# A SwiGLU encoder block on one core: the first gate/up pair with its loads by halves and an order of its own

## The chip, the cores and the metric

The kernel runs on one core of a Trainium2 chip. A core has a matrix engine (PE, TensorE), a vector engine (DVE, VectorE), a scalar engine (ACT, ScalarE), GpSimd (POOL), and SyncE (SP), which here only issues transfers (DMA). Each engine works through its own list of instructions in order; semaphores make one engine wait for another. Matrix products accumulate in PSUM banks and are read from there by VectorE or ScalarE. The metric is the device time of one execution, in microseconds, and the runs of the kernel before scatter between 2363.36 and 2370.91.

## The reference

One block of a streaming encoder, in float32: a SwiGLU feed-forward of half weight, a token mixer and a second SwiGLU feed-forward, each with a residual and a layer norm. `D_MODEL` and the sequence are 1024, the feed-forward width is 4096.

```python
def swiglu(x, w_gate, w_up, w_down):
    return (jax.nn.silu(x @ w_gate) * (x @ w_up)) @ w_down

    x = layer_norm(DN_ALPHA * x + 0.5 * swiglu(x, ffn1_w_gate, ffn1_w_up, ffn1_w_down), ln1_g, ln1_b)
    z = x @ w_in
    # fox: 8 heads of forgetting attention on z;  lru: causal convolution and a gated linear recurrence on z
    x = layer_norm(DN_ALPHA * x + concatenate([fox, lru]) @ w_out, ln2_g, ln2_b)
    x = layer_norm(DN_ALPHA * x + 0.5 * swiglu(x, ffn2_w_gate, ffn2_w_up, ffn2_w_down), ln3_g, ln3_b)
```

The part that matters here is `x @ w_gate` and `x @ w_up` at the start of both feed-forwards, FFN1 and FFN2.

## The kernel before

**Precision.** Each float32 operand is held in two parts. [...] One step of a product is three matmuls into one bank, high by high (L155), high by low (L156) and low by high (L157), in `mm3`. A low part needs its high part, so every operand passes VectorE (or a transpose on TensorE), ScalarE and VectorE again: L242/L243 for blocks of x, L293/L294 for blocks of weights.

**Products.** The feed-forwards' gate and up matrices are taken in 16 pairs of 256 columns each. For a pair, `x` (1024 x 1024) and the weights (1024 x 256) are cut into 2 x 2 blocks, and seven products of Strassen's kind (Winograd's form) replace eight: one (w11 by x11), two (w21 by x12), six (t2 by s2), five (t1 by s1), seven (t3 by s3), three (w22 by s4) and four (t4 by x22). s1 to s4 are sums and differences of blocks of x and stay for all 16 pairs; t1 to t4 are differences of weight blocks, made anew for each pair. Each product is 4 steps of 3 matmuls on 512 columns. So a pair is 14 products, seven for gate and seven for up.

**Pair 0 of FFN1.** x comes in by rows of 128 tokens, rows 0 to 3 on SP's queue, rows 4 to 7 on POOL's, each a whole row of 512 KB; then the gate and the up weights, 1 MB each, on SP. A row must be transposed on TensorE (4 transposes for half a row) before it can be a block. `blocks_1` makes the blocks "11" and "12" from rows 0 to 3. `blocks_2` makes, for each of the four groups j of tokens, s1 and "22" from row 4+j, and in a later pass s2, s3 and s4 together, each by an operation of VectorE (L260, L266, L268, L270) on what the step ahead left. It is a generator: `gate_up` advances it, and the generators of both matrices' weights, between the products, in the order one, two, five, four, six, seven, three. This order is not binding: a scheduler orders the instructions of every engine by their expected readiness.

**Buffers.** Raw weights go into two tiles (pool `rawp`), one for gate and one for up, so the load of pair 1's gate weights can be issued only when pair 0's last reader of its gate tile is through. Parts of weights take 16 tiles of pool `gu_ws`, differences 4 tiles of `gu_t`; products and transposes take turns in six PSUM banks, and two more hold running sums. Results and x's rows live in eight row tiles.

**After the pairs.** `finish` (L399 and the lines around it) multiplies gate and up of a pair, forms the seven operands of the down projection and stores them over POOL's queue; `down_ffn` then runs the down projection. FFN2 follows the mixer, its rows are the results of the second layer norm, and the transposes of "11" and "12" are spread among the mixer's last output tiles.

## Time and profile before

| what | value |
| --- | --- |
| median of 3 runs | 2370.35 us |
| the runs | 2363.36 to 2370.91 us |
| the profiled execution | 2369.74 us |
| its span | 2368.0 us |
| granted TensorE clock, mean | 0.993 |
| TensorE, busy | 2311.0 us |
| VectorE, busy | 1630.8 us |
| ScalarE, busy | 1010.8 us |
| GpSimd, busy | 224.0 us |

The profiled execution is one run of its own, 1.74 us longer than its span of instructions. A row of a view by time reads: start in us, busy us, engine, line, operation, output<-input, shapes, count, and in brackets the idle time of that engine just before it, with what ended it. Names are shortened there to their letters: `b` is a PSUM bank, `x` one of the two sum banks, `raw` a raw weight tile, `ws` a tile of `gu_ws`, `t` a difference of weights, `A` a block "11", "12" or "22", `As` a block s1 to s4, `row` one of the row tiles. A matmul's 0.39 us reaches from its start to its end in the pipeline; the next one starts 0.23 us after it.

### The profile page before, as it was taken

How to read it: one execution, taken by the hardware profiler on the slowest of the kernel's cores; microseconds unless marked ns; L12 is line 12 of the kernel's file. 1: busy time of each engine (PE TensorE's matmuls, PEld its weight loads, DVE VectorE, ACT ScalarE, POOL GpSimd, SP SyncE). 2: the span in 40 equal slices, each digit the busy share in tenths (PEclk: the TensorE clock that was granted, in tenths of full speed). 3: DMA queues.
4: the chain of work that ended last, by engine and by line, in shares of the span. 5: the costliest groups of instructions: out<-in, count | busy, mean ns of one | idle time of the engine just before them, and what ended most of it. 6: DMA issues, size and time to landing. Idle time of an engine off the chain costs nothing.

```text
span 2368.0 us, 28300 instructions
## 1 busy us (share of the span) xinstructions
PE 2311.0 (98%) x10709; PEld 1920.8 (81%) x10709; DVE 1630.8 (69%) x2512; ACT 1010.8 (43%) x1587; POOL 224.0 (9%) x368
## 2 busy tenths in 40 slices
PE   7999999999999999899999899999999999999997
PEld 6888888888788888788888787888888888788886
DVE  7766565666567786866657899766656565577787
ACT  5443433434344344454446745434333433344341
POOL 0020000000000000111133510000000000000000
PEclk9999999999999999999999999999999999999999
DMA  3433232323365432233365911423323232564532
GB/s 111 137 97 116 91 127 85 116 85 116 139 244 207 166 109 93 73 106 101 110 181 134 250 58 57 134 85 116 105 96 116 90 128 86 183 246 167 196 107 89
DMA packets 175768, 298.93 MB, mean 126 GB/s; under 512 B 8128, under 2 KB 100608, under 8 KB 175632
## 3 DMA queue, kind: packets, MB, share of 16 engines
q1 hardware_dynamic: 151984, 216.06, 28.8%
q0 software_dynamic: 23648, 81.07, 9.3%
q8 instruction: 84, 1.38, 0.2%
q14 instruction: 52, 0.43, 0.1%
HBM read 214.22 MB, written 82.87 MB: 125 GB/s over the span
## 4 chain that ended last, share of the span: by engine, by line
PE 87%; DVE 7%; issue 3%; ACT 1%; DMA 1%; POOL 1%; SPq 0%; POOLq 0%; ACTq 0%; DVEq 0%
PE x L156 9%; PE x L157 9%; PE x L155 9%; PE b L156 7%; PE b L157 7%; PE b L155 7%; PE s L157 6%; PE s L155 6%; PE s L156 6%; PE a L156 6%; PE a L157 6%; PE a L155 6%; PE a L880 1%; DMA raw<-in_ffn_w_gate_dram 1%; PE a L864 1%
## 5 line engine op out<-in xcount | busy, mean ns | idle before, releaser
L293 ACT CAST ws<-t 128x512 fp32r<-128x512 f32 x256 | 159.0, 623 | 397.8 <-PE b L156 268.7
L294 DVE TENSOR_TENSOR ws<-raw,ws 128x512 fp32r<-128x512 f32 x192 | 132.1, 688 | 145.2 <-ACT ws L293 141.8
L293 ACT CAST ws<-raw 128x512 fp32r<-128x512 f32 x192 | 118.8, 622 | 264.2 <-PE x L156 256.9
L294 DVE TENSOR_TENSOR ws<-t,ws 128x512 fp32r<-128x512 f32 x256 | 175.7, 687 | 70.4 <-ACT ws L293 68.4
L155 PE MATMUL x<-As,ws 128*128 128x512 f32 x512 | 200.0, 391 | 4.4 <-ACT As L242 4.4
L155 PE MATMUL a<-ws,ws 128*128 128x512 f32 x512 | 199.3, 391 | 3.2 <-ACT ws L487 3.2
L156 PE MATMUL a<-ws,ws 128*128 128x512 f32 x512 | 200.6, 392 | 0.6 <-DVE ws L488 0.5
L156 PE MATMUL x<-As,ws 128*128 128x512 f32 x512 | 200.2, 391 | 0.5 <-DVE As L243 0.4
L157 PE MATMUL a<-ws,ws 128*128 128x512 f32 x512 | 200.6, 392 | 0.0
L155 PE MATMUL b<-As,ws 128*128 128x512 f32 x512 | 199.7, 390 | 0.2 <-ACT row L354 0.2
L157 PE MATMUL x<-As,ws 128*128 128x512 f32 x512 | 199.9, 390 | 0.0
L157 PE MATMUL b<-As,ws 128*128 128x512 f32 x512 | 199.5, 390 | 0.0
L156 PE MATMUL b<-As,ws 128*128 128x512 f32 x512 | 199.5, 390 | 0.0
L155 PE MATMUL x<-A,ws 128*128 128x512 f32 x496 | 193.9, 391 | 4.2 <-ACT ws L293 3.9
L157 PE MATMUL x<-A,ws 128*128 128x512 f32 x496 | 193.9, 391 | 1.3 <-DVE ws L294 1.3
L156 PE MATMUL x<-A,ws 128*128 128x512 f32 x496 | 193.6, 390 | 0.0
L487 ACT CAST ws<-raw 128x1024 fp32r<-128x1024 f32 x112 | 117.3, 1049 | 174.1 <-PE a L156 90.6
L488 DVE TENSOR_TENSOR ws<-raw,ws 128x1024 fp32r<-128x1024 f32 x112 | 136.6, 1221 | 63.3 <-ACT ws L487 62.6
L409 POOL DMA_DIRECT2D h_d<-row x96 | 68.2, 713 | 1159.5 <-DVE row L403 1119.9
L155 PE MATMUL s<-ws,ws 128*128 128x512 f32 x384 | 149.6, 390 | 0.0
L157 PE MATMUL s<-ws,ws 128*128 128x512 f32 x384 | 149.6, 389 | 0.0
L156 PE MATMUL s<-ws,ws 128*128 128x512 f32 x384 | 149.5, 389 | 0.0
(232 smaller groups left out, 5206.7 us busy)
## 6 DMA issues: line engine op xcount, KB each, us to landing
raw<-h_d SPq DMA_DIRECT2D x56, 1024.0 KB, 5.5
h_d<-row POOLq DMA_DIRECT2D x96, 512.0 KB, 3.7
raw<-in_ffn_w_gate_dram SPq DMA_DIRECT2D x32, 1024.0 KB, 5.5
raw<-in_ffn_w_up_dram SPq DMA_DIRECT2D x32, 1024.0 KB, 5.5
wd<-in_ffn_w_down_dram SPq DMA_DIRECT2D x32, 1024.0 KB, 7.8
h_d<-row POOLq DMA_DIRECT2D x32, 256.0 KB, 2.6
raw<-in_w_in_dram SPq DMA_DIRECT2D x16, 512.0 KB, 5.1
row<-in_x_dram SPq DMA_DIRECT2D x12, 512.0 KB, 9.4
```

Of the source, the lines that this page charges most:

```text
L155: mm(out, ah, bh, start=first, stop=False, skip_group_check=goes_on)
L156: mm(out, ah, bl, start=False, stop=False, skip_group_check=goes_on)
L157: mm(out, al, bh, start=False, stop=last, skip_group_check=goes_on)
L293: nc.scalar.copy(hi, src)
L294: v.tensor_tensor(lo, src, f32(hi), ALU.subtract)
L409: nc.gpsimd.dma_start(d[:, 2 * n:2 * n + 2], t.rearrange("p (r t) -> p r t", r=2))
L487: nc.scalar.copy(hi, src)
L488: self.mark = v.tensor_tensor(lo, src, f32(hi), ALU.subtract)
L864: nc.tensor.transpose(pa[:, (j % 4) * P:(j % 4 + 1) * P], p[:, j * P:(j + 1) * P], self.ident)
L880: mm(pv[:, ps], vt[:, j, :], pts[h, qt][j // 4][l][:, j % 4, ps], start=j == 0 and l == 0, stop=j == last and l == 1)
```

## The change

**Loads.** For FFN1 everything now goes over SP's queue: the first halves (columns 0 to 511) of rows 0 to 3, the first halves (input rows 0 to 511) of the gate and up weights of pair 0, then the second halves of both, then rows 4 to 7 whole. Twelve transposes of the identity matrix into a bank that nobody reads stand at TensorE's start. In FFN2 the weights of pair 0 are loaded by the same two halves.

**Order.** `gate_up` has a function `first_pair` that writes pair 0 out step by step. In FFN1 it runs under `manual_schedule` for TensorE, VectorE and ScalarE: within it these three engines take their instructions in the order in which the program writes them. In FFN2 the same function runs without that and the scheduler orders it. `blocks_2` now makes s1, then s2, s3 and s4 each for all four j, one j at a time, and keeps the four transposed banks of x11 from s2 to s3. In `first_pair` w22 is made last, and t2 and t4 later than t1. In FFN1 x22's parts for j = 0, 1, 2, 3 are made after s1 of j = 0, 1, 3, 3.

**Buffers.** Rows 4 to 7 of FFN1 are in a pool of their own (`x2`), which is closed after s1; s4's block is opened in that place. The parts of w11, w21 and w22 have fixed tiles, the t21 and s tiles of `blocks_2` are eight tiles of `gu_ws`. The sum of products six and five is formed in `m.u` instead of a result row, so pair 0 takes seven row tiles where it took eight. The accumulator's rows are taken in plain order.

The diff, cut to its core:

```diff
-    def blocks_2(self, rows, bank, tmp):
+    def block_1(self, j, half, rows, bank):
+
+        self.block_parts(("11", "12")[half], j, self.transposed(rows, half, bank))
+
+    def blocks_2(self, rows, bank, t21, s):
 
         nc, v = self.nc, self.nc.vector
         r1, r2 = rows[0:4], rows[4:NT]
-        t21, s = [], []
+        a22 = []
         for j in range(4):
-            t21.append(tmp())
-            s.append(tmp())
             nc.scalar.copy(t21[j], self.transposed(r2[j], 0, bank))
-            a22 = self.transposed(r2[j], 1, bank)
-            v.tensor_tensor(s[j], a22, t21[j], ALU.add)
+            a22.append(self.transposed(r2[j], 1, bank))
+            v.tensor_tensor(s[j], a22[j], t21[j], ALU.add)
             self.block_parts("s1", j, s[j])
-            self.block_parts("22", j, a22)
-        yield
+            for k in ((0,), (1,), (), (2, 3))[j]:
+                self.block_parts("22", k, a22[k])
+            yield
+        a11 = []
         for j in range(4):
-            a11, a12 = (self.transposed(r1[j], half, bank) for half in range(2))
-            v.tensor_tensor(s[j], s[j], a11, ALU.subtract)
+            a11.append(self.transposed(r1[j], 0, bank))
+            v.tensor_tensor(s[j], s[j], a11[j], ALU.subtract)
             self.block_parts("s2", j, s[j])
-            v.tensor_tensor(t21[j], a11, t21[j], ALU.subtract)
+            yield
+        for j in range(4):
+            v.tensor_tensor(t21[j], a11[j], t21[j], ALU.subtract)
             self.block_parts("s3", j, t21[j])
+            yield
+        for j in range(4):
+            a12 = self.transposed(r1[j], 1, bank)
             v.tensor_tensor(s[j], a12, s[j], ALU.subtract)
             self.block_parts("s4", j, s[j])
             yield
 
...
+    def first_raws(self, *ws):
+
+        raws = [self.raw([P, KT, 2 * P]) for _ in ws]
+
+        def load(half):
+            ks = slice(4 * half, 4 * half + 4)
+            for r, w in zip(raws, self.gu_views(*ws)):
+                self.nc.sync.dma_start(r[:, ks, :], w[:, ks, 0:2 * P])
+
+        return raws, load
+
...
+        def first_pair(gate, up):
+
+            both = gate, up
+            b = [quarters(r) for r in raws]
+            homes = {n: [two_blocks() for _ in both] for n in ("11", "21")}
+            t21, s = ([block() for _ in range(4)] for _ in range(2))
+            blocks = self.blocks_2(rows, bank, t21, s)
+            t = {}
+
+            def fill(m, n, src):
+                k = both.index(m)
+                m.w[n] = parts(src, homes[n][k] if n in homes else None)
+
+            def steps(n):
+                for _ in range(n):
+                    next(blocks)
+
+            if later:
+                later[0](0)
+            for m, q in zip(both, b):
+                fill(m, "11", q[0])
+            gate.one()
+            for m, q in zip(both, b):
+                t["1", m] = less(q[1], q[0])
+            if later:
+                later[0](1)
+            up.one()
+            for m, q in zip(both, b):
+                fill(m, "t1", t["1", m])
+                fill(m, "21", q[2])
+            for m, q in zip(both, b):
+                t["2", m] = less(q[3], t["1", m])
+            if later:
+                gate.two()
+                steps(1)
+                up.two()
+                steps(3)
+                later[1]()
             else:
-                t2 = less(b22, t1)
-                w["t2"] = parts(t2)
-                w["t1"] = parts(t1)
-                w["t3"] = parts(less(b22, b12))
-                w["22"] = parts(b22)
-                w["t4"] = parts(less(b21, t2))
+                steps(4)
+                gate.two()
+                up.two()
+            x = bank()
+            steps(2)
+            gate.five(x)
+            fill(gate, "t4", less(b[0][2], t["2", gate]))
+            x = bank()
+            steps(2)
+            up.five(x)
+            fill(up, "t4", less(b[1][2], t["2", up]))
+            gate.four_alone()
+            steps(2)
+            fill(gate, "t2", t["2", gate])
+            up.four_alone()
+            steps(2)
+            gate.six_five()
+            fill(up, "t2", t["2", up])
+            homes["22"] = [two_blocks() for _ in both]
+            fill(gate, "t3", less(b[0][3], b[0][1]))
+            up.six_five()
+            steps(2)
+            fill(up, "t3", less(b[1][3], b[1][1]))
+            gate.seven_four()
+            steps(2)
+            up.seven_four()
+            for m, q in zip(both, b):
+                fill(m, "22", q[3])
+            for m in both:
+                m.three_alone()
 
...
                 m.six()
-                v.tensor_tensor(m.c[1], m.u, m.s5, ALU.add)
+                v.tensor_tensor(m.u, m.u, m.s5, ALU.add)
...
             def three_alone(m):
-                v.tensor_tensor(m.c[1], m.product("22", "s4"), m.c[1], ALU.add)
+                v.tensor_tensor(m.c[1], m.product("22", "s4"), m.u, ALU.add)
...
             if pair == 0:
-                blocks = self.blocks_2(rows, bank, block)
-                for x in w:
-                    next(x)
-                gate.one()
-                next(blocks)
-                gate.two()
-                up.one()
-                for x in w:
-                    next(x)
-                up.two()
-                for step in ("five", "four_alone", "six_five", "seven_four", "three_alone"):
-                    for m in (gate, up):
-                        getattr(m, step)()
-                        next(blocks, None)
-                    for x in w:
-                        next(x, None)
+                with self.tc.manual_schedule(engines=ENGINES) if later else nullcontext():
+                    first_pair(gate, up)
...
-        blk.open_blocks(xl, ("s3", "s4", "s1", "s2"))
-        rows = blk.rows()
-        for i in range(NT):
-            if i < 4:
-                nc.sync.dma_start(rows[i], xf[i * P:(i + 1) * P, :])
-            else:
-                nc.gpsimd.dma_start(rows[i], xf[i * P:(i + 1) * P, :])
-        for j in range(4):
-            blk.blocks_1(j, rows[j], bank)
-        finish = blk.gate_up(ffn1_w_gate[0], ffn1_w_up[0], h_d[0], rows, bank, tp, wsp, lambda: blk.mixer_consts(
+        blk.open_blocks(xl, ("s3", "s1", "s2"))
+        rows = [blk.row() for _ in range(4)]
+        x2 = inner.enter_context(ExitStack())
+        xp = x2.enter_context(blk.pool("x2", 4, side="right"))
+        rows += [xp.tile([P, D], F32, tag="x2", name=blk.nm("x2")) for _ in range(4)]
+
+        def open_s4():
+            x2.close()
+            blk.open_blocks(inner.enter_context(blk.pool("s4", side="right")), ("s4",))
+
+        raws, load = blk.first_raws(ffn1_w_gate[0], ffn1_w_up[0])
+        warm = bank()
+        for _ in range(12):
+            nc.tensor.transpose(warm[:, 0:P], blk.ident, blk.ident)
+        for half in range(2):
+            for i in range(4):
+                nc.sync.dma_start(rows[i][:, half * H:(half + 1) * H], xf[i * P:(i + 1) * P, half * H:(half + 1) * H])
+            load(half)
+        for i in range(4, NT):
+            nc.sync.dma_start(rows[i], xf[i * P:(i + 1) * P, :])
+
+        def block_1(half):
+            for j in range(4):
+                blk.block_1(j, half, rows[j], bank)
+
...
-        finish = blk.gate_up(ffn2_w_gate[0], ffn2_w_up[0], h_d[1], rows, bank, tp, wsp)
+        raws, load = blk.first_raws(ffn2_w_gate[0], ffn2_w_up[0])
+        load(0)
+        load(1)
```

Two places of VectorE's list in FFN1's pair 0, before and in the change. The rows of the change have the changed kernel's own line numbers: L239 and L303 are its low parts (L243 and L294 before), L253, L261, L265 and L270 the operations of s1, s2, s3 and s4 (L260, L266, L268 and L270 before), L308 a difference of weights (L299 before).

The first place is the forming of s2 and s3. VectorE before (`ws_237` and `ws_255` are the running s tiles of j = 0 and 1, `ws_236` and `ws_254` the t21 tiles, `As_18` and `As_19` are s2's high and low block, `As_12` and `As_13` s3's, `As_14` and `As_15` s4's; `b` are banks with transposed x):

```order
L266 TENSOR_TENSOR ws_237<-ws_237,b_392 128x512
L268 TENSOR_TENSOR ws_236<-b_392,ws_236 128x512
L294 TENSOR_TENSOR ws_361<-t_358,ws_360 128x512
L243 TENSOR_TENSOR As_19_121<-ws_237,As_18_120 128x4x128
L243 TENSOR_TENSOR As_13_115<-ws_236,As_12_114 128x4x128
L270 TENSOR_TENSOR ws_237<-b_397,ws_237 128x512
L266 TENSOR_TENSOR ws_255<-ws_255,b_425 128x512
L268 TENSOR_TENSOR ws_254<-b_425,ws_254 128x512
L243 TENSOR_TENSOR As_15_117<-ws_237,As_14_116 128x4x128
L243 TENSOR_TENSOR As_19_121<-ws_255,As_18_120 128x4x128
L243 TENSOR_TENSOR As_13_115<-ws_254,As_12_114 128x4x128
L270 TENSOR_TENSOR ws_255<-b_430,ws_255 128x512
```

VectorE at the same place in the change (`ws_183` to `ws_186` are the running s tiles of j = 0 to 3, `As_16` and `As_17` are s2's block, `t_423` and `t_459` are t4 of gate and up):

```order
L261 TENSOR_TENSOR ws_183<-ws_183,b_394 128x512
L239 TENSOR_TENSOR As_17_119<-ws_183,As_16_118 128x4x128
L261 TENSOR_TENSOR ws_184<-ws_184,b_402 128x512
L239 TENSOR_TENSOR As_17_119<-ws_184,As_16_118 128x4x128
L308 TENSOR_TENSOR t_423<-raw_131,t_291 128x512
L303 TENSOR_TENSOR ws_426<-t_423,ws_425 128x512
L261 TENSOR_TENSOR ws_185<-ws_185,b_430 128x512
L239 TENSOR_TENSOR As_17_119<-ws_185,As_16_118 128x4x128
L261 TENSOR_TENSOR ws_186<-ws_186,b_438 128x512
L239 TENSOR_TENSOR As_17_119<-ws_186,As_16_118 128x4x128
L308 TENSOR_TENSOR t_459<-raw_132,t_293 128x512
L303 TENSOR_TENSOR ws_462<-t_459,ws_461 128x512
```

Before, two other instructions stand between an operation and its low part; now each low part stands right behind its operation, and s2 comes as a run of four with t4 between.

The second place is the end of pair 0. VectorE before (`raw_202` and `raw_212` are pair 0's raw tiles of gate and up, `raw_641` is pair 1's of gate, `t_518` and `t_524` are t3, `x` are sums of products):

```order
L294 TENSOR_TENSOR ws_521<-t_518,ws_520 128x512
L299 TENSOR_TENSOR t_524<-raw_212 128x512
L370 TENSOR_TENSOR row_199<-row_198,row_197 128x512
L294 TENSOR_TENSOR ws_527<-t_524,ws_526 128x512
L294 TENSOR_TENSOR ws_559<-raw_202,ws_558 128x512
L370 TENSOR_TENSOR row_200<-row_198,row_197 128x512
L294 TENSOR_TENSOR ws_563<-raw_212,ws_562 128x512
L357 TENSOR_TENSOR row_199<-x_222,row_197 128x512
L374 TENSOR_TENSOR row_194<-row_194,x_222 128x512
L357 TENSOR_TENSOR row_200<-x_322,row_197 128x512
L374 TENSOR_TENSOR row_195<-row_195,x_322 128x512
L294 TENSOR_TENSOR ws_644<-raw_641,ws_643 128x512
```

VectorE there in the change (`raw_131` and `raw_132` are pair 0's raw tiles, `As_82` and `As_83` s4's block, `ws_528` and `ws_530` the low parts of gate's and up's w22):

```order
L308 TENSOR_TENSOR t_567<-raw_132 128x512
L303 TENSOR_TENSOR ws_570<-t_567,ws_569 128x512
L431 TENSOR_TENSOR row_166<-x_219,row_165 128x512
L448 TENSOR_TENSOR row_162<-row_162,x_219 128x512
L270 TENSOR_TENSOR ws_185<-b_587,ws_185 128x512
L239 TENSOR_TENSOR As_83_392<-ws_185,As_82_391 128x4x128
L270 TENSOR_TENSOR ws_186<-b_595,ws_186 128x512
L239 TENSOR_TENSOR As_83_392<-ws_186,As_82_391 128x4x128
L431 TENSOR_TENSOR row_167<-x_265,row_165 128x512
L448 TENSOR_TENSOR row_163<-row_163,x_265 128x512
L303 TENSOR_TENSOR ws_528<-raw_131,ws_527 128x512
L471 TENSOR_TENSOR row_163<-row_163,row_162 128x1024
```

Before, the last readers of the two raw tiles stand right behind t3; now they stand behind the last two operations of s4, their low parts and the additions of product seven.

The third place is SP's queue ahead of FFN2, in the change (`q`, `kh`, `kl`, `v` and `cum` are the last head's tiles of the attention, `mix` the mixer's tiles for its output projection, `raw_12055` the raw tile of FFN2's first up weights):

```order
L885 DMA q_11093<-q_d 64x1024
L886 DMA kh_11094<-k_d 64x1024
L887 DMA kl_11095<-k_d 64x1024
L888 DMA v_11096<-v_d 128x8x128
L890 DMA cum_11092<-cum_d 128x1024
L284 DMA raw_12055<-in_ffn_w_up_dram 128x4x256
L996 DMA mix_11239<-mix_d 128x1024
L996 DMA mix_11240<-mix_d 128x1024
L90 DMA gb_11243<-in_ln_g_dram 128x1024
```

Before, the two weight loads are whole and stand next to each other in front of the last head's loads (`raw_12033` and `raw_12043`, rows 166 and 167 of SP's list); now the up weights' second half stands behind the last head's loads and in front of the mix tiles.

94 lines of the change are left out of this document (45 added, 49 removed).

## The prediction

> **What bounds the kernel now.** I read the page first (busy shares, the chain of waits), then the first 110 us by windows and by time on each engine, because nearly all of the change lies in the first gate/up pair of either FFN.
>
> ```profile
> PE 2311.0 (98%) x10709; PEld 1920.8 (81%) x10709; DVE 1630.8 (69%) x2512; ACT 1010.8 (43%) x1587; POOL 224.0 (9%) x368
> PE 87%; DVE 7%; issue 3%; ACT 1%; DMA 1%; POOL 1%; SPq 0%; POOLq 0%; ACTq 0%; DVEq 0%
> core 0: us, PE busy (x) PEld busy (x) DVE busy (x) ACT busy (x) POOL busy (x), PEclk, DMA share, GB/s
> 10.00:20.00 10.00, 5.15 (x35) 4.73 (x36) 4.67 (x8) 2.78 (x6) 0.00 (x0) 0.93 0.93 322
> 20.00:30.00 10.00, 10.00 (x45) 8.16 (x44) 7.60 (x13) 6.57 (x14) 0.00 (x0) 0.90 0.01 2
> 30.00:40.00 10.00, 10.00 (x54) 8.34 (x53) 10.00 (x18) 6.24 (x12) 0.00 (x0) 1.00 0.00 0
> 40.00:50.00 10.00, 7.69 (x41) 5.92 (x39) 10.00 (x18) 6.56 (x11) 0.00 (x0) 0.97 0.00 1
> 50.00:60.00 10.00, 9.92 (x39) 7.98 (x39) 8.17 (x14) 5.85 (x9) 0.00 (x0) 0.86 0.21 57
> ```
>
> TensorE bounds the program (98%), so a change pays only where TensorE stands still. In this stage three things end its waits in turn: loads until about 17 us (DMA share 0.93), VectorE from 24 to 54 us (10.00 of 10.00 busy in two windows), and from then on TensorE itself. The landmarks on TensorE, by time:
>
> ```profile
> 17.23 0.50 PE L155 MATMUL x<-A,ws 128*128 128x512 f32 x1 [3.90 <-ACT ws L293]
> 31.90 0.39 PE L157 MATMUL b<-A,ws 128*128 128x512 f32 x1
> 32.12 0.40 PE L155 MATMUL b<-As,ws 128*128 128x512 f32 x1
> 45.77 1.04 PE L237 MATMUL b<-ident,row 128*128 128x128 f32 x8
> 49.11 1.07 PE L155 MATMUL x<-As,ws 128*128 128x512 f32 x2 [2.31 <-ACT As L242]
> 61.97 0.39 PE L155 MATMUL b<-As,ws 128*128 128x512 f32 x1
> 67.41 0.39 PE L155 MATMUL x<-A,ws 128*128 128x512 f32 x1
> 103.91 0.39 PE L155 MATMUL x<-A,ws 128*128 128x512 f32 x1
> ```
>
> 17.23 is `gate.one`, 31.90 the last matmul of `up.two`, 32.12 `gate.five`, 61.97 `gate.three_alone`, 67.41 the first product of pair 1, 103.91 that of pair 2. From 61.97 to 67.41 stand 24 matmuls, so one step is 0.227 us; a transpose is about 0.1.
>
> **The change part by part.** *Loads.* All first loads, 6.29 MB, now stand on SP's queue: first halves of rows 0 to 3, first halves of both weights, the second halves, rows 4 to 7.
>
> ```profile
> GB/s 0 236 398 410 412 412 406 381 351 349 240 0 0 0 9 0 0 0 0 0 0 0 0 0 5 0 0 0 0 9 5 0 0 205 380 289 293 32 0 0
> 19.48 1.14 ACT L293 CAST ws<-raw 128x512 fp32r<-128x512 f32 x2 [1.79 <-DMA raw<-in_ffn_w_up_dram]
> ```
>
> The slots are 1.75 us: about 410 GB/s while x is loaded, 350 in the weights, and all is there at 19.4. At these rates the pieces land by about 5.6, 8.7, 11.3, 14.3 and 19.5 us. So `gate.one` starts near 8 in place of 17.23; the second 16 transposes wait for 11.3, `up.one` ends near 16. ScalarE's strict order puts the copy of `up.one` and a t1 cast before the cast of w21, three steps or 1.6 us: `gate.two` at 17.8, and `up.two` ends at 24.8 where it ended at 32.3 (31.90 and 0.39). Up to here the change is 7.5 us ahead. The twelve added transposes lie before the first row is there and cost nothing; without that cover they are about 1.2 us.
>
> *The strict order.* Each block of x and each weight difference is made in three steps on two engines: VectorE forms it, ScalarE casts the high part, VectorE subtracts for the low part. The rows that price it:
>
> ```profile
> L243 DVE TENSOR_TENSOR As<-ws,As 128x512 fp32r<-128x512 f32 x16 | 10.5, 690 | 0.0
> 6.62 0.59 ACT L242 CAST A<-b 128x512 fp32r<-128x512 f32 x1 [0.27 <-PE b L237]
> 7.23 0.69 DVE L243 TENSOR_TENSOR A<-b,A 128x512 fp32r<-128x512 f32 x1 [0.16 <-ACT A L242]
> 44.12 0.68 DVE L266 TENSOR_TENSOR ws<-ws,b 128x512 f32<-128x512 f32 x1
> 44.72 0.69 DVE L243 TENSOR_TENSOR As<-ws,As 128x512 fp32r<-128x512 f32 x1
> 44.84 0.62 ACT L242 CAST As<-ws 128x512 fp32r<-128x512 f32 x1 [0.57 <-DVE ws L266]
> ```
>
> The first row is the group of all 16 low parts of s1 to s4 between 24.3 and 54.5 us: 0.0 us of idle before them, since other work stands between an operation and its low part. VectorE's step back to back is 0.60 us (44.12 to 44.72). In the new order the low part stands right behind its operation, so VectorE waits out the cast: 0.68 of operation, 0.04 to ScalarE (44.80 to 44.84), 0.62 cast, 0.02 back (7.21 to 7.23), 1.37 in all in place of 0.60. Each such pair loses 0.77 us and nothing fills it.
>
> First it costs the lead. For s1, VectorE runs from the end of `up.two`: the `up.two` addition and the wait for the block's copy (1.1), then for blocks 1 and 2 pairs of 1.37 and steps of 0.60, reaching the last block's operation at 30.5; its cast is there at 31.8. `gate.five` starts at 31.8, before it was 32.12: of 7.5 us, 0.3 are left.
>
> From that operation to the low part of the gate's w22, which now stands last, are 45 VectorE instructions: 45 x 0.60 = 27.0. Among them 17 are pairs of the kind above: 17 x 0.77 = 13.1. Two more waits are on others: the addition behind `up.six` waits for a product that waited for its own weights (1.3), the third s4 block's cast stands behind the table load and the silu of the gate (0.4). 30.5 + 27.0 + 13.1 + 1.7 = 72.3, and 0.1 for the last one's tail: 72.4. TensorE needs far less for it (8 products of 2.72 and 24 transposes, 24 us from 31.8), so `gate.three_alone` starts near 70.5, when s4's last cast is there, 8.5 us later than now, and its third matmul waits until 72.4.
>
> *The raw tiles.* Pair 1's gate weights go into the tile that w22 is read from.
>
> ```profile
> 56.06 0.69 DVE L294 TENSOR_TENSOR ws<-raw,ws 128x512 fp32r<-128x512 f32 x1
> 56.78 0.37 SPq L287 DMA_DIRECT2D raw<-in_ffn_w_gate_dram  x1
> 57.85 1.28 ACT L381 ACT_TABLE_LOAD   x1
> 60.77 1.06 ACT L381 ACTIVATE row<-row 128x1024 f32<-128x1024 f32 x1 [1.63 <-DVE row L374]
> 62.35 1.14 ACT L293 CAST ws<-raw 128x512 fp32r<-128x512 f32 x2 [0.53 <-DMA raw<-in_ffn_w_gate_dram]
> ```
>
> Now w22 is read at 56.06, the load issues at 56.78, the cast follows at 62.35, 5.57 later, hidden under the last four products. In the change the load issues at 72.4, the cast is at 78.0 and pair 1 begins at 78.7, while TensorE is through with `up.three_alone` at 77.8. Against 67.41 that is **+11.3 us**.
>
> *Pair 1.* VectorE comes to it late: the weights' low part stands behind two operations that wait for the load and the last product, t2's low part behind the five additions of `finish` and one of 1024 columns. I count 0.7 and 1.3 of TensorE's time: **+2.0** (between 0 and 4).
>
> *The turn to the down projection.*
>
> ```profile
> 639.98 0.58 ACT L363 COPY row<-x 128x512 f32<-128x512 f32 x1 [7.57 <-PE x L157]
> 641.56 1.19 PE L155 MATMUL a<-ws,ws 128*128 128x512 f32 x4 [1.62 <-ACT ws L487]
> ```
>
> ScalarE's order now has the cast of the first down weights before this copy, not behind it: **-1.2** (between -1.6 and 0).
>
> *The second FFN.* Its first pair gets the new sequence without the strict order; the scheduler still mixes, and VectorE's list there again has other work between an operation and its low part.
>
> ```profile
> 1424.56 0.39 PE L155 MATMUL x<-A,ws 128*128 128x512 f32 x1
> 1429.22 0.50 PE L157 MATMUL x<-A,ws 128*128 128x512 f32 x1 [1.33 <-DVE ws L294]
> 1432.88 2.38 PE L237 MATMUL b<-ident,row 128*128 128x128 f32 x20 [1.10 <-DVE row L202]
> 1437.40 0.50 PE L155 MATMUL b<-A,ws 128*128 128x512 f32 x1 [0.83 <-DVE A L243]
> 1459.66 0.72 PE L155 MATMUL x<-As,ws 128*128 128x512 f32 x2 [2.07 <-ACT As L242]
> 1460.82 0.50 PE L156 MATMUL x<-As,ws 128*128 128x512 f32 x1 [0.44 <-DVE As L243]
> 1476.84 0.39 PE L155 MATMUL x<-A,ws 128*128 128x512 f32 x1
> ```
>
> TensorE stands still 5.8 us here. The 2.07 and 0.44 are waits for s2, which the new sequence puts two products later, and 1.33 a wait for `up.one`'s low part, now made before the last normalizations; the transposes still wait for the last row, and by 1.8 more for banks. That is -3.0, and +0.5 because the up weights' second half now stands on SP between the last head's loads and the mix tiles: **-2.5** (between -5.8 and +1.5). The pools, the x2 rows' own pool and s4's late opening move no instruction on the path.
>
> **The sum**: 11.3 + 2.0 - 1.2 - 2.5 = +9.6. The profiled execution took 2369.74 us for a span of 2368.0, and the median of the runs is 2370.35, so I add it there: 2380.
>
> **The rivals.** *The lead survives.* If VectorE's casts were ready at once (nothing lost in the 17 pairs), w22 would be read 13.1 us earlier, at 59.3, pair 1 would begin near 65.6 and catch-up would be nil: -1.8 - 1.2 - 2.5, 2365. For it: ScalarE has room (6.2 to 6.6 of 10 us). Against it: every low part needs the cast of the operation just ahead, and 1.37 is the bare sum of durations. *The second FFN pays it back.* If all 5.8 us of its waits and the 1.6 of the turn go, and pair 1 catches up free, 11.3 - 1.6 - 5.8 = +3.9, 2374: no change that can be told, the bound being 0.3% or 7.1 us.
>
> ```profile
> raw<-in_ffn_w_gate_dram SPq DMA_DIRECT2D x32, 1024.0 KB, 5.5
> ```
>
> *Slow pieces.* A megabyte alone takes 5.5 us from issue to landing by this row of the page's DMA issues, 190 GB/s. If pieces in the queue ran no faster, the last row would land at 35.6, six us behind its use in the s1 chain at about 29.5: +15.6, 2386. Against it: 512 KB rows ran at 398 to 412 in the first slots. [...]
>
> **How the numbers follow.** The forecast has 0.67, the second FFN 0.17, the lead 0.08, slow pieces 0.08. The forecast's own bounds, +6 to +14, give 2376 to 2384; with the terms' ends, the FFN2 case in and most of the slow pieces, 2372 to 2387. Slower by over 0.3% means above 2377.5: the forecast but for its low end, and the slow pieces, 0.72; within 0.3% 0.20; faster 0.08.
>
> **What will show it.** Right: VectorE in 32 to 70 us some 7 of 10 us busy instead of 10, with its low parts idle on ScalarE about 0.7 us each, near 13 in all; `gate.five` near 32, `gate.three_alone` near 70, SP's load of pair 1 near 72, pair 1 near 78, pair 2 near 117. Wrong: `gate.three_alone` before 62, or low parts without idle time (then the order or the price of the cast is not what I read); `gate.one` after 12 or rows 4 to 7 after 24 (slow pieces); FFN2's first pair, from its `gate.one` to pair 1, not shorter than 52.3 by 2 to 4 us.

## Result and the profile after

The changed kernel takes 2382.27 us (median of 4 runs, 2381.01 to 2386.65) beside 2369.68 for the kernel before in the same comparison. The medians differ by 12.6 us. The ratio of the means is 1.0062 with an interval of 1.0039 to 1.0084, that is 14.7 us (9.2 to 19.9), so it is slower beyond the scatter; 2380 was predicted, with a range of 2372 to 2387. The profiled executions differ by 11.5 us in their spans (2368.0 and 2379.5).

The page after, its busy shares, and the windows of 10 to 20 and of 30 to 80 us (columns: length, then busy us and instructions of PE, PEld, DVE, ACT and POOL, then the granted clock, the DMA share and GB/s):

```profile
PE 2319.4 (97%) x10721; PEld 1922.3 (81%) x10721; DVE 1633.5 (69%) x2512; ACT 1012.9 (43%) x1587; POOL 223.1 (9%) x364
10.00:20.00 10.00, 8.29 (x40) 6.68 (x40) 5.19 (x9) 4.87 (x10) 0.00 (x0) 0.89 1.03 383
30.00:40.00 10.00, 6.85 (x21) 5.02 (x22) 7.26 (x12) 4.47 (x9) 0.00 (x0) 0.66 0.00 0
40.00:50.00 10.00, 9.01 (x41) 6.76 (x39) 6.46 (x11) 4.29 (x8) 0.00 (x0) 1.00 0.00 1
50.00:60.00 10.00, 6.91 (x28) 4.51 (x27) 6.61 (x11) 4.49 (x8) 0.00 (x0) 1.00 0.01 2
60.00:70.00 10.00, 7.83 (x36) 6.20 (x35) 6.37 (x10) 5.18 (x7) 0.00 (x0) 0.84 0.00 1
70.00:80.00 10.00, 7.32 (x20) 5.24 (x20) 6.17 (x9) 1.78 (x4) 0.00 (x0) 0.67 0.43 130
```

VectorE, which was 10.00 of 10.00 busy between 30 and 50 us, is now 6.2 to 7.3 busy in every window from 30 to 80 us, and TensorE stands still in all of them. The clock column has two windows at 0.66 and 0.67, which the kernel before has nowhere in its first 60 us. VectorE and ScalarE by time on one pair of s2, and the group of the low parts of s1 to s4 and of the weight differences between 25 and 74 us:

```profile
35.59 0.68 DVE L261 TENSOR_TENSOR ws<-ws,b 128x512 f32<-128x512 f32 x1
36.31 0.62 ACT L238 CAST As<-ws 128x512 fp32r<-128x512 f32 x1 [1.58 <-DVE ws L261]
36.96 0.69 DVE L239 TENSOR_TENSOR As<-ws,As 128x512 fp32r<-128x512 f32 x1 [0.69 <-ACT As L238]
37.57 0.68 DVE L261 TENSOR_TENSOR ws<-ws,b 128x512 f32<-128x512 f32 x1
L239 DVE TENSOR_TENSOR As<-ws,As 128x512 fp32r<-128x512 f32 x16 | 11.1, 692 | 11.3 <-ACT As L238 11.3
L303 DVE TENSOR_TENSOR ws<-t,ws 128x512 fp32r<-128x512 f32 x6 | 4.1, 689 | 3.0 <-ACT ws L302 3.0
```

From the operation to its low part (its value minus ScalarE's cast of it) are 1.37 us (35.59 to 36.96), and VectorE waits 0.69 for the cast. The group that had 0.0 of idle time before has 11.3 now.

TensorE's landmarks after, by time: gate.one, gate.two, gate.five, gate.three and its third matmul, pair 1, pair 2, the first and a later down product, FFN2's gate.one and its pair 2; then SP's load for pair 1.

```profile
9.00 0.79 PE L151 MATMUL x<-A,ws 128*128 128x512 f32 x1 [1.59 <-ACT ws L302]
19.73 0.50 PE L151 MATMUL b<-A,ws 128*128 128x512 f32 x1 [1.71 <-ACT ws L302]
33.81 0.80 PE L151 MATMUL b<-As,ws 128*128 128x512 f32 x1 [2.93 <-ACT As L238]
72.67 0.50 PE L151 MATMUL b<-As,ws 128*128 128x512 f32 x1 [1.40 <-ACT ws L302]
74.68 0.80 PE L153 MATMUL b<-As,ws 128*128 128x512 f32 x1 [1.28 <-DVE ws L303]
82.51 0.39 PE L151 MATMUL x<-A,ws 128*128 128x512 f32 x1
120.59 0.39 PE L151 MATMUL x<-A,ws 128*128 128x512 f32 x1
656.71 0.39 PE L151 MATMUL a<-ws,ws 128*128 128x512 f32 x1
657.54 0.96 PE L151 MATMUL a<-ws,ws 128*128 128x512 f32 x3 [0.45 <-ACT row L437]
1436.08 0.39 PE L151 MATMUL x<-A,ws 128*128 128x512 f32 x1
1523.39 0.39 PE L151 MATMUL x<-A,ws 128*128 128x512 f32 x1
74.65 0.38 SPq L317 DMA_DIRECT2D raw<-in_ffn_w_gate_dram  x1
```

Set beside the rows of before, the difference builds up like this. The kernel before has the first product of the down projection that goes into the bank `s` (the end of the first quarter) at 687.18 and FFN2's pair 2 at 1512.20; the changed one has them at 701.12 and 1523.39.

| stretch | predicted | measured | the difference by then |
| --- | --- | --- | --- |
| up to pair 1 (67.41, now 82.51) | +11.3 | +15.1 | +15.1 |
| pair 1 to pair 2 (103.91, now 120.59) | +2.0 | +1.6 | +16.7 |
| the other pairs of FFN1 | 0 | +0.2 | +16.9 |
| turn to the down projection, first quarter | -1.2 | -3.0 | +13.9 |
| rest of FFN1, mixer, to FFN2's gate.one (1424.56, now 1436.08) | 0 | -2.4 | +11.5 |
| first pair of FFN2, to its pair 2 | -2.5 | -0.3 | +11.2 |
| tail of the span | 0 | +0.3 | +11.5 |

A part of these differences belongs to single executions. In both profiles there are stretches in which TensorE was granted half its clock (0.50), and a step of a product takes 0.42 to 0.43 us in them instead of 0.23. Three of them in the profile of before, then two in that of the change, by windows (the clock is the third number from the end):

```profile
643.22:646.63 3.41, 3.41 (x10) 2.64 (x9) 3.41 (x4) 0.18 (x1) 0.00 (x0) 0.50 0.30 82
967.49:977.73 10.24, 7.52 (x21) 5.59 (x20) 10.24 (x21) 4.68 (x7) 0.07 (x1) 0.50 0.25 68
1203.01:1206.42 3.41, 3.14 (x7) 2.48 (x8) 2.02 (x5) 1.62 (x3) 0.93 (x2) 0.50 0.98 273
981.62:988.44 6.82, 4.08 (x12) 3.09 (x12) 6.82 (x12) 4.64 (x6) 0.00 (x0) 0.50 0.00 0
1449.24:1452.65 3.41, 3.41 (x10) 2.65 (x10) 3.41 (x7) 3.23 (x7) 0.00 (x0) 0.50 0.02 5
```

### The profile page after: what moved, and what is told of

Same layout as the page of the kernel before. It is cut to its first block, busy times and chain, and to the rows that moved or that the text cites. A ratio compares the mean times of both kernels' runs of the same rounds, so it can differ in the third digit from the quotient of the medians.

```text
span 2379.5 us, 28326 instructions
## 1 busy us (share of the span) xinstructions
PE 2319.4 (97%) x10721; PEld 1922.3 (81%) x10721; DVE 1633.5 (69%) x2512; ACT 1012.9 (43%) x1587; POOL 223.1 (9%) x364
## 4 chain that ended last, share of the span: by engine, by line
PE 89%; DVE 6%; ACT 2%; issue 2%; DMA 1%; POOL 1%; SPq 0%; POOLq 0%; ACTq 0%; DVEq 0%
PE x L153 9%; PE x L151 9%; PE x L152 9%; PE b L153 7%; PE b L151 7%; PE b L152 7%; PE s L153 6%; PE s L152 6%; PE s L151 6%; PE a L153 5%; PE a L151 5%; PE a L152 5%; PE a L938 1%; PE a L922 1%; DVE row L198 1%
## 5 line engine op out<-in xcount | busy, mean ns | idle before, releaser
L303 DVE TENSOR_TENSOR ws<-raw,ws 128x512 fp32r<-128x512 f32 x192 | 132.2, 688 | 143.6 <-ACT ws L302 140.2
L303 DVE TENSOR_TENSOR ws<-t,ws 128x512 fp32r<-128x512 f32 x256 | 175.6, 687 | 76.6 <-ACT ws L302 74.8
```

The source lines that it names most:

```text
L303: v.tensor_tensor(lo, src, f32(hi), ALU.subtract)
```

## Experiments

All times are medians beside the kernel before on the same chip; its median was 2366.6 us beside e1 to e4, 2366.7 beside e5 to e8, 2368.5 beside e9 and e10. A difference between two experiments is therefore taken from their ratios. "Pair 2" is the start of FFN1's pair 2 in the profiled execution.

| run | pair 2, us | time, us | ratio to before (interval) |
| --- | --- | --- | --- |
| the change | 120.59 | 2382.27 | 1.0062 (1.0039 to 1.0084) |
| e1, scheduler's order | 107.03 | 2365.77 | 0.9993 (0.9983 to 1.0002) |
| e2, low part later | 111.53 | 2375.38 | 1.0034 (1.0023 to 1.0045) |
| e3, w22 early | 119.14 | 2379.71 | 1.0052 (1.0038 to 1.0066) |
| e4, fill matmuls | 123.40 | 2384.46 | 1.0069 (1.0055 to 1.0083) |
| e5, FFN2 only | 104.50 | 2365.73 | 1.0000 (0.9991 to 1.0008) |
| e6, halves only | 102.30 | 2366.00 | 0.9998 (0.9989 to 1.0007) |
| e7, rows plain | 104.07 | 2367.96 | 1.0005 (0.9995 to 1.0016) |
| e8, interleaved | 100.48 | 2360.41 | 0.9974 (0.9962 to 0.9985) |
| e9, e8 with low parts at once | 111.06 | 2372.97 | 1.0019 (1.0009 to 1.0029) |
| e10, no warm-up | 122.01 | 2384.11 | 1.0064 (1.0049 to 1.0080) |

### The explicit order taken out

```diff
-                with self.tc.manual_schedule(engines=ENGINES) if later else nullcontext():
+                with nullcontext():
                     first_pair(gate, up)
```

> The changed kernel with the explicit order taken out: the same loads, tiles and steps, but the scheduler orders TensorE, VectorE and ScalarE in the first pair of FFN1, and it again puts other work between an operation and its low part. Theory (the strict order's unfilled waits for the cast cost some 13 us, and the clock falls with them): VectorE's idle time before low parts between 32 and 74 us goes from 12.3 to below 4 us, pair 2 starts near 104 to 107 instead of 120.6, and the time is 2367 to 2372. Rival (the loads by halves, the rows' own pool or the new sequence of steps cost the time): pair 2 stays near 120, 2380 to 2384.

Pair 2 starts at 107.03, 13.6 us earlier than in the change, and the time is that of the kernel before, a little under the 2367 to 2372 expected. VectorE's row for the same 16 low parts between 25 and 74 us in e1:

```profile
L239 DVE TENSOR_TENSOR As<-ws,As 128x512 fp32r<-128x512 f32 x16 | 10.8, 688 | 4.4 <-ACT As L238 4.3
```

11.3 us of idle time have become 4.4, of which 3.6 lie after 33.5 us, in two places (1.40 at 41.60 and 2.18 at 63.07). So the whole loss of time hangs on the explicit order. Loads, pools and the sequence of steps are not free in this stage even so: pair 2 is 3.1 us later than in the kernel before (103.91), which is won back behind it. What the order does is not told by this run, since TensorE and ScalarE are freed too.

### The low part one operation later

```diff
+        self.flush()
+        self.late.append(lambda: v.tensor_tensor(lo, src, f32(hi), ALU.subtract))
...
             v.tensor_tensor(s[j], s[j], a11[j], ALU.subtract)
+            self.flush()
```

> The changed kernel, its order still explicit, with one thing moved: each low part is written one VectorE operation later, so that the cast runs beside that operation. Theory (a pair costs 1.37 us in place of 0.60, 17 times): about 10 of the 17 waits go, so w22 is read about 7 to 8 us earlier, near 66; pair 2 starts 7 to 9 us earlier, near 112 to 113; 2372 to 2376. Rival (ScalarE or the transposes set the pace and the waits only move): less than 2 us, 2380 to 2383.

Pair 2 comes 9.1 us earlier, as expected, and by the ratios the time is 6.6 us shorter. Of 12.3 us of waits for casts from the last s1 on (17 places) 1.6 are left (3 places). A part of the 9.1 is the clock of this execution: it has none of the stretches at half clock (0.50) that the change has from 8.8, 66.8 and 73.7 us. VectorE's group of the additions that follow product six, between 33 and 62 us of e2, shows where the rest went: in the change it waited 1.2 us for a copied product, here 3.1.

```profile
L465 DVE TENSOR_TENSOR row<-row,row 128x512 f32<-128x512 f32 x2 | 1.4, 693 | 3.1 <-ACT row L445 3.1
```

### w22 ahead of the last two steps of s4

```diff
             fill(up, "t3", less(b[1][3], b[1][1]))
+            for m, q in zip(both, b):
+                fill(m, "22", q[3])
             gate.seven_four()
             steps(2)
             up.seven_four()
-            for m, q in zip(both, b):
-                fill(m, "22", q[3])
```

> The changed kernel with w22 of both matrices made ahead of the last two steps of s4 instead of behind them, nothing else moved: the raw tiles come free about 8 us earlier, near 66. Theory of the prediction (the late load of pair 1 is what ends last once three is late): pair 1 and 2 start 2.5 to 3 us earlier, pair 2 near 118, 2379 to 2380. Rival (TensorE's own last two products, which run at 0.43 us a step, end last, and the load was back in time): pair 1 starts at 82.5 plus or minus 0.7 as before; only the two waits inside pair 1 of 0.70 and 0.98 us go, so pair 2 near 119, and the time moves by less than 2 us.

The load for pair 1 was issued at 68.54 instead of 74.65. Pair 1 still started at 83.63, behind TensorE's own last product; only the waits inside pair 1 went, and pair 2 came 1.45 us earlier. That is nearer the rival: the late load was not what ended last. It is 0.4 us past the rival's own bound of 0.7 around 82.5. In this run all of the stage stands 0.6 us later already at gate.two (20.35 for 19.73), which accounts for half of pair 1's delay. By the ratios the time is 2.4 us shorter than that of the change, and the intervals overlap.

### Matmuls that nobody reads in the waits

```diff
+            spin(12)
             gate.five(x)
...
+            spin(6)
             for m in both:
                 m.three_alone()
```

> The changed kernel with 38 matmuls that nobody reads, put on TensorE where it waits in the first pair: 12 before gate's five, 5 and 6 before gate's and up's six, 9 before up's seven, 6 before gate's three. They fill less than the waits there (2.93, 1.18, 1.64, 2.17 and 1.40 us), so work is only added. Theory (the granted clock falls after a wait of a microsecond or two, and comes back only after some microseconds of work, so the products of this stage run at 0.43 us a step for a part of their time): with the waits filled the last 24 matmuls take 5.5 us instead of 10, pair 1 starts near 78 to 79 instead of 82.5, and the time falls by 3 to 4 us, to 2378 or 2379. Rival (the lower clock has nothing to do with the waits, or the added matmuls cost what they win): pair 1 at 82.5 or later, 2382 or more.

Nothing is won: pair 1 at 85.33, 2384.46 us. That a wait brings the clock down was the author's theory. In the change the waits of 2.93, 2.17 and 1.28 us run up to or into stretches at a clock of 0.50 (32.71 to 39.54, 66.84 to 70.26, 73.67 to 80.50), and those of 1.18 and 1.64 us lie in 27.30 us at 1.00 (39.54 to 66.84). The steps of three fell to 0.43 us for 8 of 24 matmuls, not for 12; and the slow stretches of the change at gate.five and up.seven, whose waits were filled, are gone. But gate.two and up.four, where nothing was filled, had stretches at 0.42 to 0.43 that they did not have in the change. One execution against these shifts does not price what the fill does to the clock; it shows that this fill is no remedy.

### FFN2's new pair alone

```diff
-        finish = blk.gate_up(ffn2_w_gate[0], ffn2_w_up[0], h_d[1], rows, bank, tp, wsp)
+        raws, load = blk.first_raws(ffn2_w_gate[0], ffn2_w_up[0])
+        load(0)
+        load(1)
+        finish = blk.gate_up(ffn2_w_gate[0], ffn2_w_up[0], h_d[1], rows, bank, tp, wsp, None, raws)
```

> The kernel before, with the new sequence of steps and the loads by halves in the first pair of FFN2 alone; FFN1, its loads and the accumulator's rows are as before. Theory (the prediction's term, corrected by the traces so far): from FFN2's gate.one to its pair 2 about 86.0 us in place of 87.64, so 1.6 us faster there, and the up weights' second half behind the last head's loads costs nothing; the rest as before: 2365 to 2369 beside 2366 to 2370 of the kernel before. Rival (the late up half and the mix loads behind it delay the output projection): FFN2's gate.one starts 1 to 3 us later than in the kernel before and eats the gain.

FFN2's gate.one and its pair 2 in this run:

```profile
1421.30 0.40 PE L155 MATMUL x<-A,ws 128*128 128x512 f32 x1
1507.61 0.39 PE L155 MATMUL x<-A,ws 128*128 128x512 f32 x1
```

86.3 us instead of 87.64: 1.3 won there, and gate.one is not late, so the up weights' second half behind the last head's loads cost nothing. In the time it does not show (ratio 1.0000, interval 0.9991 to 1.0008, so at most 2.1 us either way).

### The loads by halves alone

```diff
+        for half in range(2):
+            for i in range(4):
+                nc.sync.dma_start(rows[i][:, half * H:(half + 1) * H], xf[i * P:(i + 1) * P, half * H:(half + 1) * H])
+            ks = slice(4 * half, 4 * half + 4)
+            for r, w in zip(early, views):
+                nc.sync.dma_start(r[:, ks, :], w[:, ks, 0:2 * P])
+        for i in range(4, NT):
+            nc.sync.dma_start(rows[i], xf[i * P:(i + 1) * P, :])
```

> The kernel before with the new loads alone: x and the first weights by halves, rows 4 to 7 last, all on SP's queue; rows, steps and the scheduler's freedom as before. Theory (the loads are not what costs time, and alone they bring little, since VectorE and not the loads sets the pace from 24 us on): gate.one at 12 to 15 instead of 17.2, gate.five 1 to 2 us earlier than 32.1, pair 2 at 101 to 104 instead of 103.9; time within 3 us of the kernel before. Rival (smaller pieces run slower, or rows 4 to 7 come too late): rows 4 to 7 after 24 us and pair 2 at 106 or later.

```profile
31.56 0.39 PE L156 MATMUL b<-As,ws 128*128 128x512 f32 x1
102.30 0.39 PE L156 MATMUL x<-A,ws 128*128 128x512 f32 x1
```

gate.five starts 0.6 us earlier (1 to 2 were expected) and pair 2 1.6 us earlier, with no difference in the time. Without another order the earlier weights don't help, since VectorE sets the pace (9.9 to 10.0 of 10 us busy in each window from 20 to 50 us of this run); and gate.one still started at 16.29 (12 to 15 were expected), because the scheduler put the transposes of both halves ahead of it.

### The accumulator's rows in plain order

```diff
-            self.acc = self.rows()
+            self.acc = [self.row() for _ in range(NT)]
```

> The kernel before with the accumulator's rows taken in plain order (0 to 7) and nothing else. It asks where the 5 us come from that the changed kernel wins back between pair 2 of FFN1 and FFN2's gate.one. Theory A (the order of the rows: the first down weights or the output projection no longer wait): the wait of 1.62 at the turn to the down projection or those of 1.29 and 0.76 at the output projection are gone, FFN2's gate.one 1.5 to 4 us earlier, time 2363 to 2366. Theory B (the changed first pair's own buffers and the clock do it): all these waits stay, time within 1 us of the kernel before.

All three waits stay (1.62, 0.87 and 0.76 us, the second shorter than the 1.29 of before), and so does the time. Theory A is out: the rows' order is not the source of what the change wins back in the middle.

### Another explicit order

```diff
         for half in range(2):
...
+            if half == 0:
+                for i in range(4, NT):
+                    nc.sync.dma_start(rows[i], xf[i * P:(i + 1) * P, :])
...
+    def low(self, key, f):
+        self.late.append((key, f))
+        while len(self.late) > 2:
+            self.late.pop(0)[1]()
...
+            one(g)
+            T(0)
+            T(1)
+            S1(0)
+            fill(g, "t1", t["1", g])
+            one(u)
+            T(2)
+            S1(1)
+            B22(0)
+            T(3)
...
+            g.product("t1", "s1", x, True)
...
+            p["2", g] = g.product("21", "12")
```

T(j) are the transposes of row 4+j, S1(j) the operation and cast of s1, B22(j) the parts of x22; `low` keeps up to two low parts back, and each VectorE operation lets the oldest out.

> The changed kernel with another explicit order for the first pair of FFN1: a low part stands up to two VectorE operations behind its own, rows 4 to 7 are loaded ahead of the second halves, s1 and product five come before product two, w22 ahead of s4, and the copies of sums no longer stand in front of casts. FFN2 as in the change. Theory (with the round trips filled the lead of the loads is kept, and TensorE is the bound from product five on): gate.five at 22 to 24 instead of 33.8, VectorE's waits for casts behind it under 2 us in all, pair 1 at 60 to 62, pair 2 at 96.5 to 99, and with what the changed kernel wins later the time is 2355 to 2360, 8 to 11 us below the kernel before. Rival (the loads cannot keep up, or the clock falls in this stage whatever the order): pair 2 at 102 or later, 2362 or more.

TensorE's landmarks in e8 (gate.five, pair 1 and pair 2), and VectorE's groups of low parts between 25 and 62 us:

```profile
24.86 0.50 PE L151 MATMUL b<-As,ws 128*128 128x512 f32 x1 [1.24 <-DVE A L239]
63.64 0.39 PE L151 MATMUL x<-A,ws 128*128 128x512 f32 x1
100.48 0.39 PE L151 MATMUL x<-A,ws 128*128 128x512 f32 x1
L239 DVE TENSOR_TENSOR As<-ws,As 128x512 fp32r<-128x512 f32 x12 | 8.2, 682 | 0.1
L324 DVE TENSOR_TENSOR ws<-t,ws 128x512 fp32r<-128x512 f32 x6 | 4.1, 680 | 0.0
```

The waits for casts are gone (0.1 us), TensorE stands still for 0.36 us between gate.five and pair 1, and the kernel is faster than both others: 2360.41 us, 0.26% below the kernel before (interval 0.15 to 0.38%). It stayed behind the expectation by 0.9 us at gate.five, 1.6 at pair 1, 1.5 at pair 2 and 0.4 in the time, each against the upper end, and it won 6.2 us by the ratio where 8 to 11 were expected: the first two products from gate.five on took 7.4 us where 24 steps at full clock are 5.6, since the clock fell to half from 25.78 to 29.19.

### e8 with the low parts back in place

```diff
-        while len(self.late) > 2:
+        while len(self.late) > 0:
```

> The interleaved kernel e8 with one thing changed: the low part stands right behind its own operation on VectorE again, everything else (loads, steps, TensorE's and ScalarE's order) stays. It prices the disputed cost by itself. Theory (an operation and its low part cost 1.37 us together instead of 1.20 for two back to back steps, so 0.77 of idle time at each of the some 17 places, and less where TensorE waits anyway): w22 and s4 come 10 to 13 us later, pair 2 near 110 to 114 instead of 100.5, time 2370 to 2375 instead of 2360.4. Rival (the gain of e8 came from its loads and steps and not from the place of the low parts): pair 2 within 3 us of 100.5, time 2363 at most.

Nothing else differs from e8, and the groups between 25 and 74 us read:

```profile
L239 DVE TENSOR_TENSOR As<-ws,As 128x512 fp32r<-128x512 f32 x12 | 8.3, 691 | 6.9 <-ACT As L238 6.9
L324 DVE TENSOR_TENSOR ws<-t,ws 128x512 fp32r<-128x512 f32 x6 | 4.1, 689 | 3.0 <-ACT ws L323 3.0
111.06 0.39 PE L151 MATMUL x<-A,ws 128*128 128x512 f32 x1
```

6.9, 3.0 and the 0.6 of w22's parts make 10.5 us of waits at 15 places; pair 2 is 10.6 us later, and by the ratios (1.0019 and 0.9974 of about 2368) the time is 10.7 us longer (5.7 to 15.9 by the ends of the two intervals). This prices the position of the low part by itself, with what the clock does behind the waits: about 0.7 us of idle time at each place. Not each microsecond of it is on the path: a wait of VectorE for transposes, 3.41 us in e8, is 1.18 here, and against that the products of e9 up to pair 2 have 16 steps at 0.42 us or more where the clock was low, those of e8 13. The other 9.5 us that e8 wins over the change at pair 2 (120.59 to 111.06) come from the rest of its order and its loads, which no run takes apart.

### Without the twelve transposes

```diff
-        warm = bank()
-        for _ in range(12):
-            nc.tensor.transpose(warm[:, 0:P], blk.ident, blk.ident)
```

> The changed kernel without the twelve transposes of the identity at TensorE's start, nothing else. Theory (they lie before the first row is there and the clock of gate.one is not better for them: 7 of its 12 steps ran at 0.42 or 0.43 us with them): pair 2 within 1.5 us of 120.6, time within 3 us of 2382. Rival (they keep the clock up for the first products): gate.one's steps all at 0.43, up.two and with it pair 2 later by 2 us or more, 2385.

`gate.one` ran all its steps at 0.42 us or more instead of about 7 of 12, ending 1.5 us later, and pair 2 came 1.4 us later. The time is within the scatter (1.0064 beside 1.0062). Both sides have half a point: the steps did get slower, but no more than 1.4 us came of it, and another execution's clock can do as much.

## Why the prediction was right, and where its steps were not

The sign and the mechanism hold. That the size of the total holds too is in part luck, as the sum at the end shows. Step by step:

- **What bounds.** Right: VectorE from 24 to 54 us and TensorE after it. e6 shows the same from the other side, since earlier loads alone move pair 2 by 1.6 us and the time not at all.
- **Loads.** The landings were right: the window from 10 to 20 us has 383 GB/s, and no transpose of rows 4 to 7 waits for a transfer in the change. "Slow pieces" is out. gate.one was forecast at 8 and started at 9.00, gate.two at 17.8 and started at 19.73. Of this 1.0 us is the late start of gate.one, since the cast of its weights waited for their transfer until 8.33; and gate.one itself was mis-sized, about 7 of its 12 steps took 0.42 us or more. The chain that hangs on it came 1.9 us late. So of the lead of 7.5 us not 0.3 was left at gate.five but a loss of 1.7 (33.81 for 32.12).
- **The strict order.** Right in mechanism and size: 17 places were counted, 17 are in the trace, and from the start of s1's last operation (32.42) to the end of gate's low part of w22 (74.63) are 42.2 us where 41.9 were worked out. e9 confirms the price with one line of code; e2, where the low parts move, and e1, where the scheduler orders, show that most of the waits go with the position.
- **The raw tiles.** Wrong in what ends last. The forecast had pair 1 wait for its load (cast at 78.0, TensorE through at 77.8). The load was issued 2.2 us later than forecast (74.65 for 72.4), but TensorE's two last products took 10.0 us (72.67 to 82.68) where the forecast had 7.3 (70.5 to 77.8). The wait of 1.28 us for w22's low part inside them was in the forecast, with 1.9; the 13 steps at 0.42 us or more behind it, 2.8 us too long together, were not. e3 freed the tile 6 us earlier and pair 1 did not start earlier. The term for pair 1 came out at +15.1 instead of +11.3: 1.9 us stood there already at gate.two, 0.3 came in the strict order, and 1.6 behind it at gate.three.
- **Pair 1's own delay.** +1.6 for +2.0, and e3 shows its cause: with w22 early the two waits (0.70 and 0.98) are gone.
- **The turn.** The wait fell from 1.62 to 0.45 us, which is the -1.2 forecast, and it did so in e1 and e8, which have the new first pair too. The other 1.7 us of the measured 3.0 belong to the profiled execution of before, which ran at half clock from 643.22 to 646.63: e5 and e6 have the same wait of 1.62 as it has, keep the full clock behind it, and reach the next landmark 1.6 us sooner.
- **The middle.** Not foreseen: -2.4, and it is the clock of single executions and not a gain of the change. Before ran at half clock from 967.49 to 977.73 and from 1203.01 to 1206.42; the change ran so from 981.62 to 988.44, 3.42 us less, and at the second place it has almost the same waits as before (1.12 and 0.77 beside 1.29 and 0.76) and kept the full clock. The difference falls by 1.5 us across the first place and by 1.4 across the second, and 0.5 come back behind it. e5 and e6, which change only FFN2's first pair and only the first loads, have the change's pattern of the clock at both places and win 2.2 and 1.8 us; e7 has before's pattern and wins 0.4.
- **FFN2.** Mis-sized: -2.5 forecast, -0.3 in the profiled execution, -1.3 to -1.7 in e1, e2, e4 and e5. The waits fell by 2.1 us (5.77 to 3.69) and not by 3.0: those for s2 (2.51) are gone and the 1.81 of the transposes came as said, but of `up.one`'s wait of 1.33 us 0.66 stayed, and 0.34 is new. Even in the four runs 0.4 to 0.8 us less was won than the waits fell, and where it went was not followed. Behind the wait of 1.81 us the execution of the change ran at half clock (1449.24 to 1452.65) and lost 1.7 there; the other four did not. The sign that was set for this term, `gate.one` to pair 1, can't be used, since the scheduler put pair 1's first product behind twelve products of pair 0 instead of fourteen; pair 2 is taken in its place.

So the total of +9.6 came near +11.5 by luck, because errors of both signs met: 3.6 us too little up to the turn, 4.2 us not seen between the turn and FFN2, where the clock in the profile of before accounts for them, 2.2 us too much hoped for in FFN2, and 0.3 in the tail. As an estimate, without the 4.6 us of the clock at the turn and in the middle (1.7, 1.5 and 1.4) and the 1.7 in FFN2 the profiles would differ by 11.5 + 4.6 - 1.7 = 14.4 us, which is close to the 14.7 of the ratio and 5 us more than the forecast. The rival "the lead survives" is not what this order does, but what another one can do: e8 keeps the lead.

## What to carry to other kernels

An explicit order replaces the scheduler's on every engine that it names, and with it everything that the scheduler had put between dependent instructions. Before one is written out, list for each engine the pairs whose partner runs on another engine, and put one or two independent instructions between the two; here that was worth 10.7 us with a single number. Loads that came earlier paid here only together with an order that let the engine behind them use the time (e6 and e8). And before two profiles are compared stretch by stretch, look at the granted clock of both: two terms of the table above were differences of the clock.

## What the runs showed of the hardware that was not expected

A short wait does not by itself decide the granted clock: waits of nearly the same length were followed by half clock (0.50) in one run and by full clock in another, and what decides between the two is not shown. The stretches at half clock in the windows of the result section are 3.41 to 10.24 us long.

Ahead of and inside gate.three stand two waits, 1.40 and 1.28 us in the change (shown above), 1.27 and 1.29 in e2. First the windows, two in the change (one ahead of the fall and the stretch at half clock) and two in e2; then the matmuls behind the waits in the change, and the waits and what follows in e2, by time:

```profile
70.26:73.67 3.41, 1.74 (x7) 0.86 (x5) 2.73 (x5) 1.66 (x3) 0.00 (x0) 1.00 0.00 0
73.67:80.50 6.83, 5.82 (x14) 4.62 (x15) 3.71 (x6) 0.42 (x1) 0.00 (x0) 0.50 0.69 212
62.47:65.89 3.42, 2.14 (x8) 1.13 (x7) 2.99 (x6) 3.08 (x5) 0.00 (x0) 1.00 0.00 0
65.89:69.30 3.41, 2.13 (x9) 1.80 (x10) 2.96 (x5) 0.00 (x0) 0.00 (x0) 1.00 0.25 52
```

```profile
75.27 0.63 PE L151 MATMUL b<-As,ws 128*128 128x512 f32 x1
75.69 0.63 PE L152 MATMUL b<-As,ws 128*128 128x512 f32 x1
```

```profile
65.08 0.49 PE L151 MATMUL b<-As,ws 128*128 128x512 f32 x1 [1.27 <-ACT ws L320]
67.17 0.50 PE L153 MATMUL b<-As,ws 128*128 128x512 f32 x1 [1.29 <-DVE ws L321]
67.50 0.39 PE L151 MATMUL b<-As,ws 128*128 128x512 f32 x1
67.72 0.39 PE L152 MATMUL b<-As,ws 128*128 128x512 f32 x1
```

In the change the wait of 1.40 us and the beginning of that of 1.28 fall into the window from 70.26 to 73.67, TensorE is busy for 1.74 of its 3.41 us, and half clock follows. In e2 the two waits fall into the two windows, with 2.14 and 2.13 us busy, and the clock is 1.00 in both. The steps behind them are 0.42 us in the one (75.27 to 75.69) and 0.22 in the other (67.50 to 67.72). The busy time does not tell it either: in FFN2 the 3.41 us that hold the wait of 1.81 us are busy for 1.60 us in the change (from 1445.83) and in e1 (from 1431.56), and behind them a step takes 0.43 us in the change (1450.04 to 1450.47, at a clock of 0.50) and 0.23 in e1 (1435.29 to 1435.52).

So the waits alone don't give what a stage lost here. In the profile of before the stretch at half clock from 643.22 to 646.63 lies behind a wait of 1.62 us, and e5 and e6, which have the same wait and keep the full clock behind it, reach the next landmark 1.6 us sooner.
